# A fifth buffer for gathered expert rows in a one-core decoder block, paid for by rearranged SBUF

## The chip, the cores and the metric

The kernel runs on one core of one Trainium2 chip. The metric is the device time of one execution in microseconds. In the names of the profile PE is TensorE (PEld its weight loads), DVE is VectorE, ACT is ScalarE, POOL is GpSimd and SP is the engine that issues most transfers. PEq, ACTq and SPq are the sequencers of these engines.

## The reference

A decoder block for 512 tokens of width 1024. Two token mixers run side by side on the same normed input, a causal attention with 8 heads and an RWKV-7 recurrence with 8 heads; their outputs are gated and merged. After a second norm comes a mixture of 16,384 tiny experts: each token picks 16 experts for each of 8 heads, so 128 experts per token, and sums their outputs.

```python
mod = silu(c) @ w_ada + b_ada                       # shifts, scales, gates of both halves
h   = modulate(rms_norm(x), sh1, sc1)
proj = h @ w_in
o_mla  = attention(q, k, v)                         # scores + causal mask, softmax, p @ v
o_rwkv = rwkv7(...)                                 # recurrence over 512 steps, in chunks
x = x + gt1 * ((g_mla * o_mla + g_rwkv * o_rwkv) @ w_out)
h = modulate(rms_norm(x), sh2, sc2)
q = h @ w_query                                     # 8 heads, two halves
v1, i1 = top_k(q1 @ sub_keys1, 16); v2, i2 = top_k(q2 @ sub_keys2, 16)
idx, gates = top 16 of the 256 sums, softmax        # 128 experts per token
u, vv = expert_down[idx], expert_up[idx]            # rows of 1024
x = x + gt2 * sum(gates * gelu(h . u) * vv)
```

## The kernel before, in words

The 512 tokens are four blocks of 128, handled in three groups: block 0, block 1, and blocks 2 and 3 together. The first part of the program interleaves three streams: the recurrence of one group (`rwkv`), the attention of the next blocks (`mla_pre`, `mla`), and the tail of a finished group (`tail_a` to `tail_c`, then `select`, which picks the 128 experts of every token). A planner writes the instructions with priorities, and each engine then runs its own list in a fixed order. The list of VectorE is therefore decided before the kernel runs: an instruction that waits holds back everything written after it on that engine.

The experts are computed in two ways.

- **Gathered**, for blocks 0 and 1 (`peer`, L1106). In each of 256 steps GpSimd gathers for 128 tokens one row of 2048 numbers (down row and up row, 1 MB in all) into a buffer `gl`. VectorE multiplies the down half with the token's `h2p` and sums it into `z` (L1119), ScalarE applies gelu and the gate (L1120, L1121), and VectorE adds the up half to `acc` (L1125). There are `GL = 4` such buffers of 8 KB per partition: the gather of step s + 4 waits for the `acc` of step s. These steps are written with a late priority, so the planner drops them into the places where it sees VectorE free.
- **Dense**, for blocks 2 and 3. For each i of 128 rows of experts all activations z are computed as a matrix product (`dense_z`, L1162, tile `ps_z`, weights `u_raw`), multiplied by gates that are zero for unpicked experts, and multiplied by the up rows (`v_raw`) into the accumulators `acc` in PSUM. The first 40 z (`AZ + PZ`) are single products. From i = 40 on, u is split on ScalarE and VectorE into a high part `uh` and a rest `ul` (`hi_lo`, L1147), and z takes 24 matmuls; the product with v is always split and takes 12. The gates are built by `dense_spread` (L1199) in 16 steps: each writes a 1 MB tile `g_` to `gd` in DRAM on ScalarE's queue. `dense` (L1249) reads them back as `G`, one tile for 8 values of i, through `NG = 3` buffers that `g_` and `G` share.

The z from i = 40 on can start before the 128 steps of `dense` do; the names `uh`, `ul` are tiles of the pool `dz`, which is opened when the recurrence is over. The pool `de`, which holds `vh`, `vl`, `ch`, `cl` and `act`, is opened after `dense_spread`, on memory that the tiles of `dense_spread` held.

Before all this, a prologue loads two 4 MB slices of `w_ada` in eight transfers of 1 MB through the same ring `gl`, and VectorE multiplies them (L338, L340) into the scale `hA` without which the first norm cannot be finished. The table of cosines and sines (`rotary`, L377) is made there too, in the tile `rot` of a small ring `u5`.

Of the kernel before, what the change touches and what calls it, by code (L numbers as in the profile page):

```python
# [9 lines left out]
F32 = mybir.dt.float32  # L10
# [9 lines left out]
P = 128  # L20
# [9 lines left out]
GROUPS = ([0], [1], [2, 3])  # L30
DENSE = (2, 3)

GL = 4
PRE = 2
LATE = 1000
ZLATE = 100
ZFIRST = 20
AZ = 32
PZ = 8
NG = 3  # L40
BG = [[0.91, 2, 2, 1.0, 2.2, 2.85, 2.45, 1.0], [1.6, 2.28, 1, 0.58, 0.25, 0.5, 0.13, 0.36]]
ZSTEP = 2
ADA = 1
# [17 lines left out]

CST = {}
_n = 0
for _k, _w in (("ident", P), ("mM", 512), ("mOff", P), ("blk", P), ("causal", P), ("ind2", 2),
               ("sel2", P), ("invf", 16), ("invn", 3), ("invs", 24), ("iota", P)):
    CST[_k] = (_n, _n + _w)
    _n += _w
NCST = _n


def constants():
# [82 lines left out]
def _build(ctx, tc, nc, A, out):  # L154
# [86 lines left out]
        return t.rearrange("p a b -> p (a b)")  # L241


    cst = cp.tile([P, NCST], F32, name="cst")
    cols = cp.tile([P, NCOL], F32, name="cols")
    rows = mp.tile([P, NROW], F32, name="rows")
    posi = cp.tile([P, NB], I32, name="posi")
    nc.sync.dma_start(cols, A["cols"])
    nc.scalar.dma_start(cst, A["cst"])
    nc.scalar.dma_start(posi, A["pos"])  # L250

    def C(k):
        return cst[:, CST[k][0]:CST[k][1]]
# [260 lines left out]
    qT2 = pe.tile([P, 2, 8, P], F32, name="qT2", tag="gl", bufs=GL)  # L514
    G.memset(qT2[96:128], 0.0)
    p2 = pe.tile([P, 2, 512], F32, name="p2", tag="h2p", bufs=1)
    u5 = ring("u5", 512, 2, mp)

    def mla_pre(b):

# [90 lines left out]
    def mla(b):  # L611

        qT = qT2[:, b % 2]
        nk = (b + 1) * P
        ps_o = bank("ps_o", "po", 1)
        sums = small("sums", 8, pl=mp)
        ready = []
        for h in range(9):
            if h < 8:
                ps = psum_m("ps_s")  # L620
                mm(ps[:, :nk], qT[:, h, :], kT[h // 4][:, h % 4, :nk], True, False)
                mm(ps[:, nk - P:nk], ident, C("causal"), False, True)
                mx = small("mx", 1, pl=mp)
                V.tensor_reduce(mx, ps[:, :nk], axis=AX.X, op=ALU.max, negate=True)
                p_ = p2[:, h % 2]
                S.activation(p_[:, :nk], ps[:, :nk], AF.Exp, bias=mx, accum_out=sums[:, h:h + 1])
            if h:
                p_, g = ready
                ps = psum_m("ps_pT")
                for kb in range(b + 1):  # L630
                    PE.transpose(ps[:, kb * P:(kb + 1) * P], p_[:, kb * P:(kb + 1) * P], ident)
                pT = mp.tile([P, 512], F32, name="pT", tag="pT", bufs=2)
                S.copy(pT[:, :nk], ps[:, :nk])
                for kb in range(b + 1):
                    mm(ps_o[:, g * 64:(g + 1) * 64], pT[:, kb * P:(kb + 1) * P], vA[:, kb, g * 64:(g + 1) * 64],
                       kb == 0, kb == b)
            if h < 8:
                ready = p2[:, h % 2], h
            yield
        V.reciprocal(sums, sums)  # L640
        o = u5("o_")
        V.tensor_tensor(split(o, h=8), split(ps_o, h=8), bc(sums, 64, 2), op=ALU.mult)
        ps = psum_m("ps_oT")
        for j in range(4):
            PE.transpose(ps[:, j * P:(j + 1) * P], o[:, j * P:(j + 1) * P], ident)
        oT[b] = sp.tile([P, 4, P], F32, name="oT", tag="oT", bufs=3)
        S.copy(oT[b], split(ps, j=4))
        yield
# [399 lines left out]

    def select(b, tv, tp, iv, sel):

        gates = cp.tile([P, 16, 8], F32, name=f"gates{b}")
        ex = sl("ex", [P, 8, 16])
        V.tensor_tensor(ex, tv, bc(tv[:, :, 0], 16, 2), op=ALU.subtract)
        S.activation(ex, ex, AF.Exp)
        gs = small("gs", 8, pl=cp)
        V.tensor_reduce(gs, ex, axis=AX.X, op=ALU.add)
        V.reciprocal(gs, gs)
        V.tensor_tensor(gates, ex.rearrange("p h k -> p k h"), bc(gs, 16, 1), op=ALU.mult)

        tpi = tp.rearrange("p h k -> p k h").bitcast(I32)  # L1060

        def shr(n):
            t, f = sl("shi", [P, 16, 8], I32), sl("shf", [P, 16, 8])
            V.tensor_scalar(t, tpi, n, None, op0=ALU.logical_shift_right)
            V.tensor_copy(f, t)
            return f


        p4, p2 = shr(4), shr(2)
        pf, t = sl("pf", [P, 16, 8]), sl("t_", [P, 16, 8])  # L1070
        V.tensor_copy(pf, tpi)
        ab = sl("ab", [P, 2, 16, 8], BF16)
        af = sl("af", [P, 16, 8])
        V.scalar_tensor_tensor(af, p4, -16.0, pf, op0=ALU.mult, op1=ALU.add)
        V.scalar_tensor_tensor(t, p2, -12.0, p4, op0=ALU.add, op1=ALU.subtract)
        V.scalar_tensor_tensor(t, pf, 64.0, t, op0=ALU.is_ge, op1=ALU.mult)
        V.tensor_tensor(ab[:, 0], p4, t, op=ALU.add)
        V.scalar_tensor_tensor(t, p2, -4.0, pf, op0=ALU.mult, op1=ALU.add)
        V.tensor_tensor(t, t, af, op=ALU.subtract)
        V.scalar_tensor_tensor(t, pf, 64.0, t, op0=ALU.is_ge, op1=ALU.mult)  # L1080
        V.tensor_tensor(ab[:, 1], af, t, op=ALU.add)
        yield
        idx = cp.tile([P, 2, P], F32, name=f"idx{b}") if b in DENSE else sm("idx", [P, 2, P])
        for n in range(2):
            oh = b4("oh", [P, 16, 16, 8], BF16)
            V.tensor_tensor(oh, bc(ab[:, n], 16, 1), bc(iota16, 16, 2), op=ALU.is_equal)
            V.tensor_tensor(oh, oh, bc(iv[:, n], 16, 2), op=ALU.mult)
            for w in (8, 4, 2):
                V.tensor_tensor(oh[:, :w], oh[:, :w], oh[:, w:2 * w], op=ALU.add)
            V.tensor_tensor(idx[:, n].rearrange("p (k h) -> p k h", k=16), oh[:, 0], oh[:, 1], op=ALU.add)  # L1090
            yield
        gf = gates.rearrange("p k h -> p (k h)")
        if b in DENSE:
            sel[b] = idx, gf
            yield
            return
        V.scalar_tensor_tensor(idx[:, 0], idx[:, 0], 128.0, idx[:, 1], op0=ALU.mult, op1=ALU.add)
        ii = cp.tile([P, P], I32, name=f"ii{b}")
        V.tensor_copy(ii, idx[:, 0])
        sel[b] = ii, gf  # L1100
        yield
# [60 lines left out]
    def dense_z(i):  # L1162
# [13 lines left out]
        if i < AZ + PZ:  # L1176
            zs = ((u, dn["hf"]),)
        else:
            uh = dz.tile([P, D], F32R, name="uh", tag="uh", bufs=2)
            ul = dz.tile([P, D], F32R, name="ul", tag="ul", bufs=2)  # L1180
            hi_lo(uh, ul, u)
            zs = ((uh, hh_), (uh, hl_), (ul, hh_))
        ps = bank("ps_z", "pr", 3)
# [65 lines left out]
    def dense(sel):  # L1249
# [19 lines left out]
        for i in range(P + 1):  # L1269
            if i < P:  # L1270
                if i % SUB == 0:
                    gates_of(i // SUB + 2)
                    if AZ <= i + SUB < AZ + PZ:
                        t = dn["z"].tile([P, SUB, nd], F32, name="A", tag="A", bufs=AZ // SUB)
                        nc.sync.dma_start(t, zd[:, i + SUB - AZ:i + 2 * SUB - AZ])
                        for j in range(SUB):
                            dn["act"][i + SUB + j] = t[:, j]
# [181 lines left out]
```

## Time and profile before

| | us |
|---|---|
| median of 3 runs | 1945.18 (1934.06 to 1948.34) |
| the profiled execution | 1931.73 |
| its span, first to last instruction | 1930.0 |
| PE busy in the span | 1712.6 (89%) |
| DVE busy in the span | 1597.4 (83%) |
| ACT busy in the span | 702.8 (36%) |
| mean DMA rate | 308 GB/s |

The rows further down come from that one execution. Times in them are microseconds from the start of the span; durations at the end of a group row are nanoseconds where the row says "mean". A busy PE is modelled: two matmuls in flight overlap, so the distance from one start to the next tells more than the duration.

### The profile page before, as it was taken

To read this page: it belongs to the slowest core of one execution; us is meant where nothing else is said; L and a number is where in the kernel's file an instruction comes from. 1 tells how busy PE (TensorE), PEld (TensorE's weight loads), DVE (VectorE), ACT (ScalarE), POOL (GpSimd) and SP (SyncE) were. 2 spreads that over 40 slices of the span, in tenths; PEclk is the share of its full clock that TensorE was granted. 3 is DMA by queue.
4 is the path that set the end of the run, shared out by engine and by line. 5 is a ranking of instruction groups with operands and counts; after the bars stand their busy time and mean duration, and the time that the engine had idled before them with its cause. 6 is when DMAs were issued, how large, how long until landed. Compare 5 with 4: busy or idle time off the path is not lost.

```text
span 1930.0 us, 30268 instructions
## 1 busy us (share of the span) xinstructions
PE 1712.6 (89%) x11002; PEld 1465.1 (76%) x11002; DVE 1597.4 (83%) x3724; ACT 702.8 (36%) x1727; POOL 447.9 (23%) x394
## 2 busy tenths in 40 slices
PE   2889999999899999994769868978899999999998
PEld 2667777778787798883458857766689989988897
DVE  6675546458778898887789999977899999999997
ACT  1244233321323322231131123343465555555553
POOL 1210010000232200333322224310133433233230
PEclk9999999899999999996989988998999999999999
DMA  7744755166987975988989978998999999999995
GB/s 299 261 155 146 240 171 181 33 222 211 371 334 266 346 237 180 337 307 301 372 346 354 342 286 307 364 343 331 404 382 404 415 413 415 416 415 413 415 398 201
DMA packets 152642, 595.03 MB, mean 308 GB/s; under 512 B 13854, under 2 KB 47902, under 8 KB 117548
## 3 DMA queue, kind: packets, MB, share of 16 engines
q1 hardware_dynamic: 76768, 287.22, 40.3%
q0 software_dynamic: 39360, 280.51, 37.7%
q10 hardware_dynamic: 36364, 25.36, 4.2%
q8 instruction: 86, 1.41, 0.3%
q14 instruction: 64, 0.52, 0.1%
HBM read 569.96 MB, written 23.09 MB: 307 GB/s over the span
## 4 chain that ended last, share of the span: by engine, by line
issue 31%; PE 28%; DMA 14%; POOL 13%; DVE 12%; ACT 1%; POOLq 0%; SPq 0%; DVEq 0%; ACTq 0%
POOL gl L1116 13%; DMA gl<-in_experts,ii 6%; PE ps_b L234 4%; PE ps_q L234 3%; DMA w_b<-in_w_b 3%; PE ps_gt L234 3%; DVE acc L1125 2%; DVE gl L1119 2%; DMA w_out<-in_w_out 2%; PE ps_m L234 2%; PE ps_ap L234 2%; PE ps_mix L234 2%; DMA w_ada<-in_w_ada 2%; PE ps_y L234 1%; PE ps_s L234 1%
## 5 line engine op out<-in xcount | busy, mean ns | idle before, releaser
L1116 POOL DMA_INDIRECT gl<-in_experts,ii x256 | 393.6, 1537 | 988.5 <-DVE acc L1125 727.1
L1119 DVE SCALAR_TENSOR_TENSOR gl<-gl,h2p 128x1024 f32<-128x1024 f32 x256 | 311.2, 1216 | 51.6 <-DMA gl<-in_experts,ii 51.2
L1125 DVE SCALAR_TENSOR_TENSOR acc<-gl,z,acc 128x1024 f32<-128x1024 f32 x256 | 326.5, 1275 | 5.8 <-ACT z L1121 5.1
L234 PE MATMUL acc<-vh,ch 128*128 128x512 f32 x512 | 198.0, 395 | 11.1 <-ACT ch L1148 9.8
L234 PE MATMUL acc<-vl,ch 128*128 128x512 f32 x512 | 203.0, 397 | 4.3 <-DVE vl L1149 4.3
L234 PE MATMUL acc<-vh,cl 128*128 128x512 f32 x512 | 203.8, 398 | 2.6 <-DVE cl L1149 2.4
L234 PE MATMUL ps_z<-hh,ul 128*128 128x256 f32 x704 | 199.5, 283 | 2.4 <-DVE ul L1149 2.4
L234 PE MATMUL ps_z<-hh,uh 128*128 128x256 f32 x704 | 199.4, 283 | 0.4 <-ACT act L1188 0.4
L234 PE MATMUL ps_z<-hl,uh 128*128 128x256 f32 x704 | 199.6, 283 | 0.0
L1120 ACT ACTIVATE z<-z 128x1 f32<-128x1 f32 x256 | 51.9, 203 | 389.1 <-DVE gl L1119 389.0
L234 PE MATMUL ps_z<-hf,u_raw 128*128 128x256 f32 x640 | 160.2, 391 | 12.6 <-ACT i1T L1222 12.6
L1149 DVE TENSOR_TENSOR vl<-v_raw,vh 128x1024 fp32r<-128x1024 f32 x128 | 156.1, 1219 | 7.8 <-ACT vh L1148 7.6
L234 PE MATMUL ps_gt<-hT,w_b 128*128 128x128 f32 x1024 | 135.2, 285 | 9.8 <-DMA w_b<-in_w_b 7.3
L234 PEld LDWEIGHTS ps_z<-hf,u_raw 128*128 128x128 f32 x640 | 116.9, 195 | 31.6 <-ACT i1T L1222 13.0
L1148 ACT CAST vh<-v_raw 128x1024 fp32r<-128x1024 f32 x128 | 134.1, 1048 | 16.2 <-DMA v_raw<-in_dense 10.1
L234 PEld LDWEIGHTS ps_z<-hh,uh 128*128 128x128 f32 x704 | 134.6, 191 | 7.0 <-issue 3.1
L234 PEld LDWEIGHTS ps_gt<-hT,w_b 128*128 128x128 f32 x1024 | 126.0, 199 | 16.2 <-issue 11.1
L234 PEld LDWEIGHTS ps_z<-hl,uh 128*128 128x128 f32 x704 | 134.8, 192 | 3.1
L234 PEld LDWEIGHTS ps_z<-hh,ul 128*128 128x128 f32 x704 | 134.7, 191 | 2.7 <-DVE ul L1149 2.6
L234 PE MATMUL ps_b<-hT,w_b 128*128 128x128 f32 x896 | 123.2, 287 | 13.9 <-DMA w_b<-in_w_b 11.0
L234 PEld LDWEIGHTS ps_b<-hT,w_b 128*128 128x128 f32 x896 | 112.5, 199 | 24.4 <-issue 12.8
L234 PE MATMUL ps_q<-h2T,w_q 128*128 128x128 f32 x1024 | 125.5, 277 | 1.2 <-DMA w_q<-in_w_query 1.1
(432 smaller groups left out, 3308.5 us busy)
## 6 DMA issues: line engine op xcount, KB each, us to landing
u_raw<-in_dense SPq DMA_DIRECT2D x128, 512.0 KB
v_raw<-in_dense SPq DMA_DIRECT2D x128, 512.0 KB
w_b<-in_w_b SPq DMA_DIRECT2D x90, 512.0 KB
w_q<-in_w_query SPq DMA_DIRECT2D x48, 512.0 KB
w_ada<-in_w_ada SPq DMA_DIRECT2D x32, 512.0 KB
G<-gd SPq DMA_DIRECT2D x16, 1024.0 KB
w_o<-in_w_o SPq DMA_DIRECT2D x24, 512.0 KB
w_out<-in_w_out SPq DMA_DIRECT2D x24, 512.0 KB
```

The source lines that it names most:

```text
L234: PE.matmul(o, l, r, start=start, stop=stop)
L1116: G.indirect_dma_start(out=gl, out_offset=None, in_=A["experts"], in_offset=bass.IndirectOffsetOnAxis(ap=ii[:, s:s + 1], axis=0))
L1119: V.scalar_tensor_tensor(gl[:, :D], gl[:, :D], 1.0, h2, op0=ALU.mult, op1=ALU.mult, accum_out=z[:, 0:1])
L1120: S.activation(z[:, 1:2], z[:, 0:1], AF.Gelu_apprx_tanh)
L1125: V.scalar_tensor_tensor(acc, gl[:, D:], z[:, 1:2], acc, op0=ALU.mult, op1=ALU.add)
L1148: S.copy(hi, x)
L1149: V.tensor_tensor(lo, x, hi.bitcast(F32), op=ALU.subtract)
```

## The change

- The ring `gl` gets five buffers in place of four.
- The 8 KB for it come from the pool `mp` of the attention: the scratch rings `u5` (2 x 2 KB) and `pT` (2 x 2 KB) are gone. Their place is a tile `x5` in the ring `gl` itself, cut into four quarters of 2 KB; two serve as `u5`, two as `pT`. Like the keys and values of the attention, `x5` frees its buffer for gathers when the attention is over.
- The mask `causal` moves from the constants that are kept to a tile of `mp`, with a transfer of its own.
- Gates and indices of blocks 2 and 3 move from the lasting pool to `dz`.
- `uh` and `ul` move from `dz` to `de`.
- `G` and `g_` get two buffers in place of three, and the gates of group j + 1 are asked for at the start of group j, where before those of group j + 2 were.

```diff
-GL = 4
+GL = 5
...
-NG = 3
+NG = 2
...
+NKEPT = CST["causal"][0]
...
-    cst = cp.tile([P, NCST], F32, name="cst")
+    cst = cp.tile([P, NKEPT], F32, name="cst")
+    causal = mp.tile([P, P], F32, name="causal")
...
-    nc.scalar.dma_start(cst, A["cst"])
+    nc.scalar.dma_start(cst, A["cst"][:, :NKEPT])
     nc.scalar.dma_start(posi, A["pos"])
+    nc.scalar.dma_start(causal, A["cst"][:, NKEPT:])
...
-    u5 = ring("u5", 512, 2, mp)
+    x5 = pe.tile([P, 4, 512], F32, name="x5", tag="gl", bufs=GL)
+    turn5 = {"u": 0, "p": 0}
+
+    def half5(kind, shape=None):
+        at = {"u": 0, "p": 2}[kind] + turn5[kind] % 2
+        turn5[kind] += 1
+        t = x5[:, at]
...
+    def u5(name, shape=None):
+        return half5("u", shape)
...
-                mm(ps[:, nk - P:nk], ident, C("causal"), False, True)
+                mm(ps[:, nk - P:nk], ident, causal, False, True)
...
-                pT = mp.tile([P, 512], F32, name="pT", tag="pT", bufs=2)
+                pT = half5("p")
...
-        gates = cp.tile([P, 16, 8], F32, name=f"gates{b}")
+        home = dn["z"] if b in DENSE else cp
+        gates = home.tile([P, 16, 8], F32, name=f"gates{b}")
...
-            uh = dz.tile([P, D], F32R, name="uh", tag="uh", bufs=2)
-            ul = dz.tile([P, D], F32R, name="ul", tag="ul", bufs=2)
+            uh = dn["v"].tile([P, D], F32R, name="uh", tag="uh", bufs=2)
+            ul = dn["v"].tile([P, D], F32R, name="ul", tag="ul", bufs=2)
...
-                    gates_of(i // SUB + 2)
+                    if i:
+                        gates_of(i // SUB + 1)
```

The planner's order moves with it. Three places show how. The first is VectorE in the prologue, from the last multiplication of the first `w_ada` slice to the first row of the recurrence's input (`sh`). Before:

```order
L344 TENSOR_TENSOR hB<-ps_mod,cols 128x8
L398 TENSOR_SCALAR rot<-rot 128x64
L338 TENSOR_SCALAR part<-w_ada,sc 128x1024
L397 TENSOR_TENSOR rot<-rot 128x64
L340 SCALAR_TENSOR_TENSOR part<-w_ada,sc,part 128x1024
...
L407 SCALAR_TENSOR_TENSOR sn<-rot 128x4x16
L408 TENSOR_SCALAR sn<-sn 128x4x16
L340 SCALAR_TENSOR_TENSOR part<-w_ada,sc,part 128x1024 x6
L346 TENSOR_TENSOR hA<-ps_mod,cols 128x8
```

and in the changed kernel, where the table is made in `x5`:

```order
L347 TENSOR_TENSOR hB<-ps_mod,cols 128x8
L341 TENSOR_SCALAR part<-w_ada,sc 128x1024
L343 SCALAR_TENSOR_TENSOR part<-w_ada,sc,part 128x1024 x5
L386 TENSOR_SCALAR x_232<-cst,posf 128x16 x4
...
L349 TENSOR_TENSOR hA<-ps_mod,cols 128x8
...
L411 TENSOR_SCALAR sn<-sn 128x4x16
L507 TENSOR_TENSOR sh<-pr 128x128
```

The table's instructions stood between the multiplications and ahead of `hA`; now 38 of its rows lie between `hA` and `sh`.

The second place is VectorE at the end of the selection for block 3, just ahead of the first step of `dense_spread` (`iota`, then the comparisons `o`). Before:

```order
L1090 TENSOR_TENSOR idx_8753<-oh 128x128
L1089 TENSOR_TENSOR oh<-oh 128x1024
L1211 CAST iota<-cst 128x256
L1089 TENSOR_TENSOR oh<-oh 128x512
L1223 CAST gb<-gT 128x128
L1089 TENSOR_TENSOR oh<-oh 128x256
```

and in the changed kernel:

```order
L1108 TENSOR_TENSOR idx_8681<-oh 128x128
L1107 TENSOR_TENSOR oh<-oh 128x1024
L1137 SCALAR_TENSOR_TENSOR gl,z<-gl,h2p 128x1024
L1107 TENSOR_TENSOR oh<-oh 128x512
L1143 SCALAR_TENSOR_TENSOR acc<-gl,z,acc 128x1024
L1107 TENSOR_TENSOR oh<-oh 128x256
L1137 SCALAR_TENSOR_TENSOR gl,z<-gl,h2p 128x1024
L1108 TENSOR_TENSOR idx_8681<-oh 128x128
L1143 SCALAR_TENSOR_TENSOR acc<-gl,z,acc 128x1024
L1229 CAST iota<-cst 128x256
```

Two whole gather steps stand now where none stood. Counted over VectorE's list up to the first comparison `o`, 129 gather steps are finished before and 135 now.

The third place is the queue of SP where `dense` starts. Before:

```order
L1282 DMA v_raw<-in_dense 128x1024 x4
L1175 DMA u_raw<-in_dense 128x1024 x24
L1282 DMA v_raw<-in_dense 128x1024
L1262 DMA G<-gd 128x2048 x3
L1282 DMA v_raw<-in_dense 128x1024
L1262 DMA G<-gd 128x2048
L1282 DMA v_raw<-in_dense 128x1024 x3
```

and in the changed kernel:

```order
L1301 DMA v_raw<-in_dense 128x1024 x4
L1193 DMA u_raw<-in_dense 128x1024 x20
L1301 DMA v_raw<-in_dense 128x1024
L1280 DMA G<-gd 128x2048 x2
L1301 DMA v_raw<-in_dense 128x1024
L1193 DMA u_raw<-in_dense 128x1024
L1280 DMA G<-gd 128x2048
L1301 DMA v_raw<-in_dense 128x1024
L1280 DMA G<-gd 128x2048
```

Four loads of `u_raw` fewer stand ahead of the first `G`, and two `G` are asked for together in place of three.

## Rows read from the trace of the kernel before

**Rows 1.** Busy time by stage: start:end, length, engines (instructions), clock, DMA share, GB/s

```profile
480.00:660.00 180.00, 164.56 (x1122) 138.36 (x1120) 143.18 (x308) 57.05 (x176) 48.39 (x58) 0.97 0.87 331
660.00:860.00 200.00, 194.05 (x1473) 175.30 (x1474) 176.01 (x564) 58.89 (x182) 42.68 (x40) 1.00 0.75 268
860.00:1010.00 150.00, 96.54 (x501) 72.38 (x500) 119.03 (x238) 35.75 (x117) 50.79 (x37) 0.81 0.89 335
1010.00:1165.00 155.00, 121.77 (x790) 111.31 (x789) 147.32 (x548) 30.51 (x93) 36.59 (x30) 0.91 0.87 321
1165.00:1310.00 145.00, 124.42 (x948) 105.90 (x948) 126.70 (x196) 55.54 (x132) 44.91 (x16) 0.94 1.01 348
1310.00:1450.00 140.00, 131.25 (x561) 104.96 (x562) 127.15 (x191) 71.38 (x130) 27.40 (x19) 0.96 0.97 373
1450.00:1880.00 430.00, 427.36 (x2713) 385.08 (x2712) 424.12 (x558) 237.18 (x472) 150.31 (x86) 1.00 1.02 412
```

**Rows 2.** Instructions of PE in order of time, late in the dense stage

```profile
1871.53 0.40 PE L234 MATMUL acc<-vh,ch 128*128 128x512 f32 x1
...
1874.29 0.28 PE L234 MATMUL ps_z<-hh,uh 128*128 128x256 f32 x1
...
1877.15 0.40 PE L234 MATMUL acc<-vh,ch 128*128 128x512 f32 x1
```

**Rows 3.** VectorE's gate products in order of time: one for each i

```profile
1508.31 0.41 DVE L1287 SCALAR_TENSOR_TENSOR act<-act,G 128x256 f32<-128x256 f32 x1
1513.59 0.41 DVE L1287 SCALAR_TENSOR_TENSOR act<-act,G 128x256 f32<-128x256 f32 x1
1520.02 0.41 DVE L1287 SCALAR_TENSOR_TENSOR act<-act,G 128x256 f32<-128x256 f32 x1
```

**Rows 4.** VectorE's groups, 1500 to 1850: count | busy us, mean ns | idle before

```profile
L1125 DVE SCALAR_TENSOR_TENSOR acc<-gl,z,acc 128x1024 f32<-128x1024 f32 x70 | 89.2, 1274 | 0.0
L1119 DVE SCALAR_TENSOR_TENSOR gl<-gl,h2p 128x1024 f32<-128x1024 f32 x70 | 85.0, 1215 | 5.5 <-DMA gl<-in_experts,ii 5.5
```

**Rows 5.** VectorE's waits, 480:660, 660:860, 860:1010, 1010:1165: total us, times, longest

```profile
DVE gl L1119 <- DMA gl<-in_experts,ii: 12.6, 11, 2.3
DVE gl L1119 <- DMA gl<-in_experts,ii: 8.3, 5, 2.8
DVE gl L1119 <- DMA gl<-in_experts,ii: 11.7, 8, 3.9
DVE gl L1119 <- DMA gl<-in_experts,ii: 7.7, 5, 2.7
```

**Rows 6.** PE's waits, 860 to 1010: total us, times, longest

```profile
PE ps_ynT L893 <- DVE y L887: 18.1, 1, 18.1
```

**Rows 7.** VectorE in the prologue, in order of time, with idle time before

```profile
33.46 7.88 DVE L340 SCALAR_TENSOR_TENSOR part<-w_ada,sc,part 128x1024 f32<-128x1024 f32 x6
45.01 0.17 DVE L346 TENSOR_TENSOR hA<-ps_mod,cols 128x8 f32<-128x8 f32 x1 [3.66 <-PE ps_mod L234]
45.21 0.17 DVE L347 TENSOR_TENSOR hA<-hA,cols 128x8 f32<-128x8 f32 x1
51.58 0.29 DVE L504 TENSOR_TENSOR sh<-pr 128x128 f32<-128x128 f32 x1 [6.21 <-ACT pr L500]
```

**Rows 8.** Busy time by stage in the prologue

```profile
25.00:30.00 5.00, 3.57 (x16) 3.49 (x16) 1.74 (x9) 0.00 (x0) 0.00 (x0) 1.00 1.02 396
35.00:40.00 5.00, 0.00 (x0) 0.00 (x0) 4.89 (x4) 0.00 (x0) 3.04 (x2) 1.00 0.65 264
```

**Rows 9.** ScalarE's queue of transfers from 1174 to 1207, to 1210, to 1213: packets, MB

```profile
q10 hardware_dynamic: 7925, 4.03, 40.7%
q10 hardware_dynamic: 8118, 4.13, 38.2%
q10 hardware_dynamic: 9421, 4.79, 40.9%
```

**Rows 10.** ScalarE in `dense_spread`: fourth write, and first copy of sixth step

```profile
1196.46 1.43 ACTq L1246 DMA_DIRECT2D gd<-g__9001  x1
1207.71 1.07 ACT L1245 COPY g__9138<-ps_G 128x512 f32<-128x512 f32 x2 [3.95 <-PE ps_igT L1221]
```

**Rows 11.** The start of `dense`: last write of gates, first reads, first product

```profile
1292.62 0.52 ACTq L1246 DMA_DIRECT2D gd<-g__9836  x1
1307.09 1.76 SPq L1262 DMA_DIRECT2D G<-gd  x3
1313.07 0.80 PE L234 MATMUL acc<-vh,ch 128*128 128x512 f32 x1 [9.50 <-ACT ch L1148]
```

More of the change, by code (lines that the diff above doesn't have):

```diff
@@ L63 @@
 _n = 0
-for _k, _w in (("ident", P), ("mM", 512), ("mOff", P), ("blk", P), ("causal", P), ("ind2", 2),
-               ("sel2", P), ("invf", 16), ("invn", 3), ("invs", 24), ("iota", P)):
+for _k, _w in (("ident", P), ("mM", 512), ("mOff", P), ("blk", P), ("ind2", 2),
+               ("sel2", P), ("invf", 16), ("invn", 3), ("invs", 24), ("iota", P), ("causal", P)):
     CST[_k] = (_n, _n + _w)
@@ L516, in _build @@
     p2 = pe.tile([P, 2, 512], F32, name="p2", tag="h2p", bufs=1)
-    u5 = ring("u5", 512, 2, mp)
+    x5 = pe.tile([P, 4, 512], F32, name="x5", tag="gl", bufs=GL)
[4 more added lines that the diff above has]
+        t = x5[:, at]
+        if shape is None:
+            return t
+        n = math.prod(shape[1:])
+        assert n <= 512
+        return t[:, :n] if len(shape) == 2 else t[:, :n].rearrange("p (a b) -> p a b", a=shape[1])
+    def u5(name, shape=None):
+        return half5("u", shape)
     def mla_pre(b):
@@ L1082, in select @@
         yield
-        idx = cp.tile([P, 2, P], F32, name=f"idx{b}") if b in DENSE else sm("idx", [P, 2, P])
+        idx = home.tile([P, 2, P], F32, name=f"idx{b}") if b in DENSE else sm("idx", [P, 2, P])
         for n in range(2):
```

## The prediction

> **What bounds the kernel now.** I read the busy time by stage first, because one average over 1930 us says nothing about a program whose stages differ. From 480 to 1165 us the recurrence, the tails and the first gathers are interleaved; from 1165 to 1310 the gates are built; from 1310 on the dense product runs beside the remaining gathers [rows 1]. In the last stage PE, VectorE and the transfers all look full: 427 and 424 of 430 us, and 412 GB/s [rows 1]. A busy PE is modelled, so I then read PE in order of time. One i of the dense stage takes 12 matmuls from 1871.53 to 1874.29, then 24 from 1874.29 to 1877.15, and the next i begins at once [rows 2]: 2.76 + 2.86 = 5.62 us with no gap. The stage itself holds 2713 matmuls in 430 us, at 36 for each i 75.4 of them, so 5.70 us for one i [rows 1]. **The dense stage from i = 40 on runs at PE's own pace**, within 1.5%. VectorE is close behind: it takes 5.28 us for an i with one gather step and 6.43 us for one with half a step more [rows 3]. So a gather step costs VectorE about 2 x 1.15 = 2.3 us of its time, less than the sum of the two durations [rows 4] since instructions overlap.
>
> Earlier it is otherwise. From 860 to 1165 PE has large holes (96.5 of 150 us, 121.8 of 155) while VectorE has 119 and 147 [rows 1], and PE once waits 18.1 us for a VectorE instruction of the recurrence that stands behind gather steps [rows 6]. From 660 to 860 PE is at 194 of 200. Waits of VectorE for gathered rows, which is what a fifth buffer can shorten, come to 12.6, 8.3, 11.7 and 7.7 us in the four stages, 40.3 together [rows 5]; between 1500 and 1850 they are 5.5 us [rows 4].
>
> **The change part by part**, against the profiled execution, which took 1931.7 us. The median of the three runs shown is 13.5 us, or 0.7%, longer; I put the sum on that median.
>
> *Prologue.* The last six multiplications by `w_ada` run back to back from 33.46 to 41.34, `hA` follows at 45.01 [rows 7], while the transfers have already dropped from 396 to 264 GB/s [rows 8]. VectorE is late there, not the loads. The table's rows leave the way: some 30 of them stood between the first multiplication and this burst, at about 0.13 us each, so 4 us. They return behind `hA`, where VectorE now sits idle for 6.21 us [rows 7]; 38 rows at 0.13 are 4.9 us and fit. If they take 0.23 us each because every one needs the one before, they are 8.7 and stick out by 2.5. I take **-4**, between -6 and +3. With the fifth buffer the loads are also asked for earlier; since VectorE is the late one, nothing more.
>
> *Waits for gathered rows.* With five buffers each gather is asked for one `acc` earlier, some 5 us at the pace of the last stage. The longest waits are 2.3 to 3.9 us [rows 5], so one step of lead covers most of them, unless the transfers themselves are the limit: in a run of gather steps VectorE takes one each 2.3 us, and 1.05 MB at the 321 to 335 GB/s of these stages [rows 1] takes 3.2. Five buffers then cover one step more of such a run and no more. Before 860 PE is nearly full and VectorE's waits hardly show: I take 2 of the 20.9 us there, and 12 of the 19.4 behind it: **-14**. Ends: 0 and -40.
>
> *Gather steps that move forward.* Up to the first step of the gate building VectorE's list holds 135 finished steps in place of 129, and twelve in place of thirteen during it. Six steps are 13.8 us. Three of the six come before the query stage, where VectorE has 31 us of holes in 150 [rows 1] but is also the one PE waits for [rows 6]: I count half, 3.5. The other three come where it is nearly full: 6.9. One fewer in the gate building: -2.3. Together **+8**, between 0 and +13.8.
>
> *Gates in two buffers.* A write of 1 MB to `gd` is 2048 pieces of 512 bytes. After 1174 ScalarE's queue had moved 8118 pieces by 1210 and 9421 by 1213 [rows 9]; four writes are 8192. So the fourth write, asked for at 1196.46, landed just after 1210, 13.5 us later, while the first copy of the sixth step came at 1207.71 [rows 10]. With two buffers that copy needs the fourth write's buffer and waits 2.3 us or more. There are 14 such reuses. A step that starts late gives the next write more time, ScalarE is idle for most of a step, and VectorE's two sets of operands run ahead; I take **+4**. Ends: 0, and 16 (every second reuse, none absorbed). At the start of `dense` the first reads wait for the last write, from 1292.62 to 1307.09 [rows 11], with two buffers as with three; group 2 is asked for when group 0 has been used and is needed after the fourth product, which at 2.76 us each leaves some 10 us. Nothing for that.
>
> *Split rows in the later pool.* `uh` and `ul` now lie on memory that the gate building still holds, so products with split rows can't start during it. In PE's list 113 of these matmuls stood ahead of the first `acc` product, and now 38 do. The 75 others filled the hole before 1313.07 [rows 11] and cost nothing; now they come at i = 41 to 43, in the stage that runs at PE's pace: 75 x 2.86 / 24 [rows 2] = **+9**. They cost 0 if PE has slack there, which rows 2 speak against.
>
> *Dense stage.* VectorE's last gather step stands at i = 116 in place of 124, as nine steps more are done when i = 44 is reached. At PE's pace that gives only 8 x (5.70 - 5.62) = **-1**. Ends: -1, and -21 (nine steps at 2.3, if VectorE set the pace). *Mask, constants, x5 in place of two rings:* the scratch keeps two halves of each kind, and PE's order there is the same row for row: 0.
>
> Sum: -4 - 14 + 8 + 4 + 9 - 1 = **+2**, so 1947 on the median's scale.
>
> A rule of the skill bears on the last-but-one term. The Trainium skill (Perfetto Trace Analysis, "Identifying the Most-Contended Engine") says that matmul busy time is a poor measure of how near PE is to its limit, and that the share of weight loads is one to use instead. That share is 385 of 430 us, or 90% [rows 1], which by the rule leaves PE a tenth of slack where VectorE, at 424, has none; the sum would then be that of the first rival. I side with the start-to-start distances [rows 2].
>
> **The rivals.**
>
> *VectorE, not PE, sets the dense stage.* For it: 424 of 430 us busy, and an i with a step and a half takes 6.43 us, longer than PE's 5.62. Against it: PE's gapless starts. Then nine steps fewer are worth 20.7 us in place of 1: 2 - 20 = -18, so 1927. Chance 0.12.
>
> *The waits for rows vanish altogether,* because one buffer more takes each fetch off VectorE's path and PE's holes between 860 and 1165 close with them: -40 in place of -14, so -24 and 1921. Against it: PE is full from 660 to 860, and the runs of steps are fed at 3.2 us each. Chance 0.08.
>
> *Slower: the gate writes hold back ScalarE.* ScalarE's list holds the gelu of the gathered steps behind the copies into `g_`; a copy that waits for a write holds back `z`, and so `acc` on VectorE, which feeds the gate building itself. It decides if a write takes longer than the 11 us or so between its issue and the copy two steps on; rows 9 and 10 show 13.5. With the waits for rows limited by the transfers (0 in place of -14) and 16 in place of 4, the sum is -4 + 0 + 8 + 16 + 9 - 1 = +28, so 1973. Chance 0.17.
>
> *The fifth buffer does nothing,* since five fetches in flight only share the same rate: -4 + 0 + 8 + 4 + 9 - 1 = +16, so 1961. Chance 0.20.
>
> **How the numbers follow.** My forecast has the remaining 0.43: gains and losses that nearly cancel. It is the likeliest, so 1947 is the predicted time. The range takes in the first two rivals' nearer half and the fourth with its worse ends: 1921 to 1970; what lies outside is most of the third (0.14) and some of the second (0.05). About 1% (19 us) is what a measurement can tell from no change: faster than that is the second rival, half of the first, and a little of the forecast's own spread: 0.17. Slower is the third and a little of the fourth: 0.20. Within 1%: 0.63.
>
> **What the profile afterwards would show.** `hA` at about 41 us in place of 45, `sh` at 47 or 48. VectorE's waits for gathered rows from 480 to 1165 at 25 us or less in place of 40. The first `acc` product of `dense` within 5 us of 1313. Start to start on PE still 5.62 us for an i at 1500 and at 1870, and no faster after the last gather step: if an i gets shorter there, VectorE was the limit. The interleaved stage begins at i = 41 and lasts about 9 us longer. ScalarE's copies into `g_` would for the first time wait for the queue of writes. I am wrong if PE turns out to have slack in the dense stage, if the holes from 860 to 1165 close by more than 15 us, or if the gate building takes over 15 us longer than its 145.

## The result, and the profile after

The change runs in 1958.1 us against 1938.9 (medians of 17 runs each). Over all these runs the ratio is **1.009, with a 95% interval of 1.0069 to 1.0111**, so some 17 us slower. The profiled execution of the change took 1964.2 us, at the slow end of its runs (1943 to 1965), the one of before 1931.7, at the fast end of its own (1926 to 1952). Row against row the two differ by 32.5 us, and nearly half of that is the choice of the executions; so below each reading is checked against further profiles.

Busy time by stage of the changed kernel (start:end, length, PE, PEld, DVE, ACT, POOL with instructions, clock, DMA share, GB/s), which answers to [rows 1]:

```profile
480.00:660.00 180.00, 159.90 (x1038) 135.84 (x1038) 135.74 (x307) 52.48 (x162) 50.94 (x56) 0.91 0.82 316
660.00:860.00 200.00, 191.49 (x1426) 171.65 (x1425) 169.40 (x560) 57.10 (x175) 40.92 (x38) 0.97 0.71 251
860.00:1010.00 150.00, 98.90 (x538) 74.56 (x537) 121.38 (x225) 30.92 (x111) 54.27 (x39) 0.80 0.92 359
1010.00:1165.00 155.00, 137.83 (x907) 126.66 (x906) 153.00 (x569) 40.89 (x120) 41.52 (x36) 0.96 0.96 362
1165.00:1310.00 145.00, 108.47 (x806) 90.92 (x806) 130.09 (x220) 46.43 (x120) 39.91 (x17) 0.88 0.92 313
1310.00:1450.00 140.00, 117.43 (x516) 92.05 (x515) 122.72 (x184) 66.79 (x124) 30.00 (x20) 0.91 0.97 368
1450.00:1880.00 430.00, 425.08 (x2689) 380.52 (x2688) 424.36 (x559) 239.10 (x473) 134.33 (x84) 1.00 1.02 413
```

The dense stage is as full as it was. From 480 to 860 PE and VectorE are both busy for less time, at a lower granted clock: that is where this execution fell behind. From there on the windows no longer hold the same work, since everything lies some 25 us later.

VectorE's waits for gathered rows over the whole kernel (total us, times), before and now:

```profile
  DMA gl<-in_experts,ii: 51.2, 42
  DMA gl<-in_experts,ii: 8.5, 7
```

By stage, to set beside [rows 5] (total, times, longest), only 480 to 660 and 860 to 1010 have any; 660 to 860 and 1010 to 1165 have none:

```profile
DVE gl L1137 <- DMA gl<-in_experts,ii: 6.4, 5, 2.3
DVE gl L1137 <- DMA gl<-in_experts,ii: 0.3, 1, 0.3
```

So the fifth buffer did to these waits far more than the prediction gave it (25 us or less left, of 40), and yet the kernel is slower. What grew are other waits. PE's waits for weights from 480 to 1010 added up to 22.1 us before (total, times, longest):

```profile
PE ps_mix L234 <- DMA w_out<-in_w_out: 9.9, 4, 3.1
PE ps_m L234 <- DMA w_o<-in_w_o: 8.0, 3, 3.1
PE ps_gt L234 <- DMA w_b<-in_w_b: 3.1, 3, 2.2
PE ps_q L234 <- DMA w_q<-in_w_query: 1.1, 1, 1.1
```

and now make 38.3:

```profile
PE ps_mix L235 <- DMA w_out<-in_w_out: 12.6, 5, 6.2
PE ps_gt L235 <- DMA w_b<-in_w_b: 11.0, 7, 2.8
PE ps_m L235 <- DMA w_o<-in_w_o: 7.3, 4, 3.7
PE ps_b L235 <- DMA w_b<-in_w_b: 4.0, 2, 2.8
PE ps_q L235 <- DMA w_q<-in_w_query: 3.4, 1, 3.4
```

PE's longest single wait, the 18.1 us of [rows 6], grew as well:

```profile
PE ps_ynT L910 <- DVE y L904: 21.9, 1, 21.9
```

It is 17.8 to 18.1 us in all seven profiles with four buffers and 21.9 to 23.3 in all seven with five. During this wait VectorE starts five multiplications by `h2p` and seven additions to `acc` with four buffers, and eight of each with five: its waits for rows there, 1.0 to 1.3 us with four buffers, are gone in five of the seven with five, but more gather steps stand ahead of the `y` that PE needs.

The prologue answers to [rows 7]: `hA` at 41.79 in place of 45.01, `sh` at 47.92 in place of 51.58.

```profile
41.79 0.17 DVE L349 TENSOR_TENSOR hA<-ps_mod,cols 128x8 f32<-128x8 f32 x1 [3.30 <-PE ps_mod L235]
47.92 0.29 DVE L507 TENSOR_TENSOR sh<-pr 128x128 f32<-128x128 f32 x1 [0.73 <-ACT pr L503]
```

PE in the dense stage, to set beside [rows 2]: an i begins with its first `acc` product, early, and again after VectorE's last gather step, which ended before 1890.

```profile
1499.00 0.40 PE L235 MATMUL acc<-vh,ch 128*128 128x512 f32 x1
...
1504.58 0.40 PE L235 MATMUL acc<-vh,ch 128*128 128x512 f32 x1
...
1899.72 0.40 PE L235 MATMUL acc<-vh,ch 128*128 128x512 f32 x1
...
1905.31 0.40 PE L235 MATMUL acc<-vh,ch 128*128 128x512 f32 x1
```

5.58 us and 5.59 us: **PE's own pace, no faster when VectorE has nothing else to do.**

To compare many profiles I divide the end of the kernel at four VectorE instructions: the cast of the last top-k (`iv`), the first comparison `o` of the gate building, the first gate product `A` of `dense`, and the last addition into `y`. For the change:

```profile
1150.90 0.23 DVE L1054 CAST iv<-i 128x32 bf16<-128x32 uint32 x1
1189.55 0.74 DVE L1252 TENSOR_TENSOR o<-iota,i2T 128x1024 f16<-128x1024 f16 x1
1339.33 1.43 DVE L1306 SCALAR_TENSOR_TENSOR A<-A,G 128x256 f32<-128x256 f32 x4 [8.39 <-DMA G<-gd]
1957.33 1.28 DVE L1330 TENSOR_TENSOR y<-y,x2e 128x512 f32<-128x512 f32 x2
```

and for the kernel before, in a second profile of it (its run took 1945.6 us):

```profile
1139.23 0.23 DVE L1037 CAST iv<-i 128x32 bf16<-128x32 uint32 x1
1176.02 0.69 DVE L1234 TENSOR_TENSOR o<-iota,i2T 128x1024 f16<-128x1024 f16 x1
1323.08 1.10 DVE L1287 SCALAR_TENSOR_TENSOR A<-A,G 128x256 f32<-128x256 f32 x3 [4.84 <-DMA G<-gd]
1938.65 1.29 DVE L1311 TENSOR_TENSOR y<-y,x2e 128x512 f32<-128x512 f32 x2
```

The stretches in all profiles, in us (the ratio is to before, with its interval; "steps" are the gather steps that VectorE's list holds ahead of the first `o`, and those between the first and the last `o`, both counted by their `acc`; the prediction's count of the first is one lower):

| kernel | ratio | steps | `iv` at | to `o` | to `A` | to the end | last three |
|---|---|---|---|---|---|---|---|
| before | 1 | 130, 13 | 1129.8 | 36.7 | 145.6 | 612.7 | 795.0 |
| before, again | | 130, 13 | 1139.2 | 36.8 | 147.1 | 615.6 | 799.4 |
| e4 split rows alone | 1.0033 (1.0007 to 1.0059) | 130, 14 | 1138.1 | 35.0 | 144.9 | 622.8 | 802.7 |
| e3 two gates alone | 1.0064 (1.0033 to 1.0094) | 132, 13 | 1142.3 | 41.3 | 148.1 | 614.1 | 803.5 |
| e6 the same again | 1.0049 (1.0014 to 1.0084) | 132, 13 | 1143.2 | 40.8 | 149.5 | 614.1 | 804.4 |
| e1 change with four buffers | 1.0088 (1.0052 to 1.0125) | 132, 14 | 1149.7 | 39.7 | 148.2 | 617.0 | 804.9 |
| change | 1.0090 (1.0069 to 1.0111) | 136, 13 | 1150.9 | 38.6 | 149.8 | 618.0 | 806.4 |
| e8 change, again | | 136, 13 | 1147.8 | 38.6 | 144.8 | 621.9 | 805.3 |
| e2 change, split rows back | 1.0088 (1.0052 to 1.0124) | 136, 13 | 1139.0 | 38.7 | 156.4 | 607.9 | 803.0 |
| e5 fifth buffer alone | 1.0032 (0.9996 to 1.0068) | 134, 13 | 1144.9 | 34.3 | 152.5 | 610.2 | 797.0 |
| e11 change, 9 steps held | 1.0011 (0.9979 to 1.0044) | 136, 4 | 1138.0 | 38.6 | 123.1 | 629.7 | 791.4 |
| e9 fifth buffer, 10 held | 0.9982 (0.9953 to 1.0011) | 134, 3 | 1137.9 | 34.3 | 114.6 | 636.2 | 785.0 |
| e10 fifth buffer, 5 held | 0.9982 (0.9954 to 1.0010) | 134, 8 | 1144.6 | 34.3 | 116.7 | 628.7 | 779.7 |
| **e12 before, 5 held** | **0.9947 (0.9918 to 0.9977)** | 130, 8 | 1130.0 | 35.8 | 117.3 | 632.4 | 785.5 |

Two things are to be seen at once. Up to `iv` the lists of before, e3, e4, e6 and e12 are the same, and their `iv` still lies anywhere from 1129.8 to 1143.2: a difference of less than 13 us there, between single profiles, says nothing. After `iv` the repeats agree within 5 us, and there the parts of the change can be read off, if they are larger than that. The three stretches after `iv` make 797.0 us in e5, as in before (795.0 and 799.4): with nearly nothing but the fifth buffer changed, no loss shows there.

### The profile page after: what moved, and what is told of

It is laid out like the page before. It is cut to its first block, busy times and chain, and to the rows that moved or that the text cites. A ratio compares the mean times of both kernels' runs of the same rounds, so it can differ in the third digit from the quotient of the medians.

```text
span 1962.5 us, 30290 instructions
## 1 busy us (share of the span) xinstructions
PE 1726.5 (88%) x11002; PEld 1476.2 (75%) x11002; DVE 1598.5 (81%) x3724; ACT 704.4 (36%) x1727; POOL 435.5 (22%) x394
## 5 line engine op out<-in xcount | busy, mean ns | idle before, releaser
L1134 POOL DMA_INDIRECT gl<-in_experts,ii x256 | 378.9, 1480 | 954.3 <-DVE acc L1143 698.4
L235 PE MATMUL ps_z<-hf,u_raw 128*128 128x256 f32 x640 | 160.3, 391 | 19.3 <-ACT i1T L1240 18.1
L235 PE MATMUL ps_b<-hT,w_b 128*128 128x128 f32 x896 | 131.5, 299 | 16.0 <-DMA w_b<-in_w_b 14.1
L235 PEld LDWEIGHTS ps_b<-hT,w_b 128*128 128x128 f32 x896 | 120.8, 211 | 26.1 <-issue 9.9
```

The source lines that it names most:

```text
L235: PE.matmul(o, l, r, start=start, stop=stop)
L1134: G.indirect_dma_start(out=gl, out_offset=None, in_=A["experts"], in_offset=bass.IndirectOffsetOnAxis(ap=ii[:, s:s + 1], axis=0))
```

## The experiments

**Which part costs.** Four kernels, timed against before on one chip.

e1, the change with four buffers for rows:

```diff
-GL = 5
+GL = 4
-    x5 = pe.tile([P, 4, 512], F32, name="x5", tag="gl", bufs=GL)
+    x5 = pe.tile([P, 4, 512], F32, name="x5", tag="x5", bufs=1)
```

> The change with four buffers for gathered rows; the attention's scratch keeps its 8 KB in a buffer of its own, all else as in the change. The lists of the engines are those of the kernel before up to the gate building, apart from the rotary table. Theory A (the fifth buffer itself costs time: the gathers that are fetched ahead hold back the weight loads that PE waits for between 480 and 860 us, and more gather steps lie in stages in which PE is full): most of the loss goes, the ratio to before is 1.002 to 1.005 (about +5 to +9 us, the split rows and the gates remain), and PE's waits for weights from 480 to 1010 us are back at some 22 us from 38. Theory B (the loss comes from what had to make room: split rows, gates in two buffers, scratch): ratio 1.008 to 1.010 as for the whole change.

Measured: 1.0088 (1.0052 to 1.0125), the whole loss. **Theory A falls and theory B holds**: without the fifth buffer the change is as slow as with it, to within some 8 us. The run takes back more than the waits: the table stands again where it stood before (`hA` at 45.36), and the four gather steps that the fifth buffer moves ahead of `o` are back. What theory A said of the weights came true all the same: PE's waits for weights from 480 to 1010 fall back from 38.3 to 24.6 us:

```profile
PE ps_mix L235 <- DMA w_out<-in_w_out: 9.4, 3, 5.9
PE ps_gt L235 <- DMA w_b<-in_w_b: 8.3, 6, 2.1
PE ps_m L235 <- DMA w_o<-in_w_o: 5.4, 3, 2.6
PE ps_q L235 <- DMA w_q<-in_w_query: 1.5, 1, 1.5
```

and VectorE's waits for rows are back at 47.5 us. Over all profiles, PE's waits for weights up to 1165 are 34 to 44 us in the seven with four buffers and 51 to 56 in the seven with five, while VectorE's for rows are 44 to 55 and 4 to 10. The fifth buffer removes some 40 us of waits from one engine and puts 14 on the other, besides the 4 us of PE's longest wait, and the time does not fall.

e2, the change with the split rows in the earlier pool again:

```diff
-            uh = dn["v"].tile([P, D], F32R, name="uh", tag="uh", bufs=2)
-            ul = dn["v"].tile([P, D], F32R, name="ul", tag="ul", bufs=2)
+            uh = dz.tile([P, D], F32R, name="uh", tag="uh", bufs=2)
+            ul = dz.tile([P, D], F32R, name="ul", tag="ul", bufs=1)
```

> The change with the split rows uh and ul in the pool of the gate building again (ul with one buffer, so that they fit). 98 split-row products stand ahead of the first acc product in place of 38. If the split rows cost PE time in the dense stage, 60 x 2.86 / 24 = 7 us come back: ratio to before 1.005 to 1.006 in place of 1.009. If PE has slack there, 1.009 as before. Rival: the split rows are worth the whole loss (some 20 us), ratio 1.000.

Measured: 1.0088 (1.0052 to 1.0124), nothing gained. The table shows why: the stretch after `A` is 10 to 14 us shorter, and the one before it 7 to 12 longer. What the split products save in the dense stage, the gate building loses. The split products do not do that by themselves: the kernel before has 113 of them ahead of the first `acc` product and e4 has 38, and their gate building takes the same time. `ul` has one buffer in e2, and over the whole kernel VectorE waits 6.4 us, in ten waits, to write `ul` until PE has finished a `ps_z` product, a wait that before does not have; it was not tried apart.

e3 and e6, gates of two groups alone, which were timed twice:

```diff
-NG = 3
+NG = 2
...
-                    gates_of(i // SUB + 2)
+                    if i:
+                        gates_of(i // SUB + 1)
```

> The kernel before with gates of two groups in place of three and nothing else. If ScalarE's copies into g_ wait for the queue of writes and hold back the gate building: +4 to +16 us, ratio 1.002 to 1.008. If the two sets of operands of VectorE take up the wait: 1.000, and the gate building keeps its 145 us.

> Gates of two groups alone a second time, since its ratio was known to 0.3% only and its trace shows 2 to 4 us in the gate building where the times say 12. If the term is what the trace shows: 1.002 to 1.004. If it is what the first times said: 1.006.

Measured: 1.0064 (1.0033 to 1.0094) and 1.0049 (1.0014 to 1.0084). **Two gates are the largest part of the loss by these numbers**, though the intervals overlap that of e4 below. ScalarE in order of time in the second of them: the write of a step, and the copies two steps on that need its buffer.

```profile
1206.27 0.52 ACTq L1246 DMA_DIRECT2D gd<-g__8933  x1
1213.07 1.07 ACT L1245 COPY g__9001<-ps_G 128x512 f32<-128x512 f32 x2 [6.53 <-DMA gd<-g__8865]
1214.84 1.07 ACT L1245 COPY g__9001<-ps_G 128x512 f32<-128x512 f32 x2
1215.95 0.52 ACTq L1246 DMA_DIRECT2D gd<-g__9001  x1
1221.99 1.07 ACT L1245 COPY g__9069<-ps_G 128x512 f32<-128x512 f32 x2 [6.07 <-DMA gd<-g__8933]
```

The write asked for at 1206.27 holds the copy at 1221.99: 15.7 us. There are nine such waits, 36.5 us of ScalarE's time; in the two profiles of before there are none and one (3.4 us), and the copy in [rows 10] waited for PE. But the gate building is only 2.4 us longer (148.8 against 146.4, means of two), less than the 5 us by which two profiles of one kernel can differ. The other part stands ahead of it: the stretch from `iv` to `o` is 41 us in place of 36.8, since the planner puts two gather steps more there (132 in place of 130 ahead of the first `o`). 4.3 us for two steps is 2.2 each.

e4, the split rows in the accumulation's pool alone (the diff of e2 on the kernel before, the other way round, with two buffers for both `uh` and `ul`):

> The kernel before with the split rows uh and ul in the accumulation's pool and nothing else: 38 split-row products ahead of the first acc product in place of 113. If PE sets the pace of the dense stage: 75 x 2.86 / 24 = +9 us, ratio 1.0046. If PE has slack there or the last products only fill the same holes: 1.000. Rival: more than 9 (ratio over 1.007), if VectorE's splits of these rows, which come behind the gate building too, are on the path as well.

Measured: 1.0033 (1.0007 to 1.0059), so 1 to 11 us. After `A` the profile has 622.8 us in place of 612.7 and 615.6, +9. The means of e3 and e6 and of e4 add up to 1.009, the 1.0088 of e1: nothing is left over for the scratch in `x5` and the moved mask, which were not tried apart.

e5, the fifth buffer nearly alone: the change with the edit of e2, that of e3 the other way round, and

```diff
-            act = dz.tile([P, nd], F32, name="zp", tag="zp", bufs=2)
+            act = dz.tile([P, nd], F32, name="zp", tag="zp", bufs=1)
```

> The change with gates of three groups and the split rows in the gate building's pool again, so that the fifth buffer (and what goes with it: the scratch in it, the rotary table behind hA, the gather steps moved forward) stands nearly alone; to make it fit, ul and zp have one buffer each. The change against the same with four buffers was 1.0090 against 1.0088. If the fifth buffer is worth nothing and the loss is all in what made room: ratio to before 1.000, between 0.998 and 1.002, gate building (first comparison o to first product with A) at 146 us or less. If two gates cost what their own run says and the split rows nothing in company: 1.002. If the fifth buffer itself costs: 1.006 or more. If it gains once nothing is given up for it: below 0.996.

Measured: 1.0032 (0.9996 to 1.0068). This lies between the case in which the buffer is worth nothing and the one in which it costs, and excludes a gain of more than 0.04%. With two gates and the late split rows taken back, the fifth buffer still earns nothing. But `zp` with one buffer is a price of its own, which PE does not pay in before:

```profile
PE ps_z L235 <- ACT zp L1206: 5.7, 2, 5.0
```

The expected shorter gate building did not show (152.5 us), and this wait, which lies in it, may be part of the reason.

**How much of a profile is the change's.**

> The kernel before once more, for a second profile. If the 23 us by which the first comparison o came later in the changed kernel's profile (1189.5 against 1166.5) are the clock's run-to-run variation, this profile has o anywhere from 1166 to 1184, with dips of the granted clock in other places. If they are the change's: o at 1166 to 1169 again.

> The changed kernel once more, for a second profile. If the loss before the gate building is the change's: first comparison o at 1186 or later again. If it is mostly the clock of that one execution: between 1170 and 1184.

Measured: `o` at 1176.0 and at 1186.4. Both statements hold in part: 23 us between the first two profiles become 10 between the second two. Of these, 2 are the shorter or longer stretch after `iv`; the rest lies ahead of `iv`, where seven profiles with five buffers have a mean of 1143.3 and six with four buffers and the list of before 1137.1, with a spread of about 5 us in each. The 6 us between the means are some two standard errors.

**Where a gather step is free.** If a step ahead of the dense stage costs 2.3 us and PE sets the pace behind it, steps should be held back until then. One small VectorE instruction does it: it copies a mark, made when the last operands of the gate building are, into the tile that the held step writes next.

```diff
+                        if q == len(sel) - 1 and t0 + h0 + HB == n:
+                            dn["built"] = dn["z"].tile([P, 1], F16, name="built")
+                            V.tensor_copy(dn["built"], og[:, 0, 0, 0, 0:1])
...
                 z = pl.tile([P, 2], F32, name="z", tag="z", bufs=4)
+                if b * P + s == HOLD:
+                    V.tensor_copy(z[:, 0:1], dn["built"])
```

On e5, HOLD = 137:

> The fifth buffer nearly alone (as in the run before, ratio 1.003), with one instruction more: gather step 137 waits on VectorE until the last operands of the gate building are made, so that 3 gather steps lie in the gate building in place of 13, and the last gather step stands at i = 126 in place of 118. Theory C (gather steps that lie ahead of the dense stage cost VectorE 2.3 us each, those in the dense stage nothing as long as PE sets its pace): the gate building is 10 x 2.3 = 23 us shorter; 84 split-row matmuls that it hid come back in the dense stage, 84 x 2.86 / 24 = 10 us; net -13, ratio to before 0.996 to 0.998. Rival (VectorE has slack in the gate building, PE or ScalarE sets it): gate building as long as before, ratio 1.008. Rival (VectorE sets the dense stage too): the 23 come back there, ratio 1.003 to 1.008.

On e5, HOLD = 142:

> The same with step 142 held: 8 gather steps in the gate building in place of 13, 68 split-row matmuls fewer ahead of the first acc product, last gather step at i = 122. Theory C: 5 x 2.3 = 11.5 us off the gate building, 8 us back in the dense stage: ratio 1.001 to 1.002. Rivals as for ten steps: 1.006, or 1.003.

On the change, HOLD = 140:

> The whole change with step 140 held: 4 gather steps in the gate building in place of 13, last gather step at i = 124 in place of 115; 25 split-row matmuls fewer ahead of the first acc product. Theory C: 9 x 2.3 = 21 us off the gate building, 3 back in the dense stage, net -18: ratio to before 1.000 in place of 1.009. If the copies into g_ wait for the writes in two buffers whatever VectorE does: no more than half of it, 1.005. If VectorE has slack in the gate building: 1.009 or more.

Measured: 0.9982 (0.9953 to 1.0011), 0.9982 (0.9954 to 1.0010) and 1.0011 (0.9979 to 1.0044). **Theory C holds in its direction**: the change loses 15 us of its 17 by this one instruction, though it keeps two gates and the late split rows; expected were 18. With two gates held steps help no less, so the waits of ScalarE's copies were not the bound there. On e5, from 1.0032, ten held steps bring 10 us where 10 to 14 were expected, and five bring as much, where 2 to 4 were. The hold takes more steps out of the way than was counted: between the first `o` and the first `A` VectorE has 17 in e5 and in the change, but 10 in e10 and 4 in e9 and e11, so seven and thirteen fewer. That it is the steps which count, and not the split products that fall out with them, e4 bears out: it has 75 products fewer ahead of the first `acc` product, one step more, and no shorter gate building.

On the kernel before, HOLD = 138:

> The kernel before, with its four buffers, and step 138 held until the gate building's last operands are made: 8 gather steps in the gate building in place of 13, 89 split-row matmuls fewer ahead of the first acc product (24), last gather step at i = 126 in place of 123. It tells what the fifth buffer adds to the held steps (0.9982 with both). Theory C: 5 x 2.3 = 11.5 us off the gate building, 89 x 2.86 / 24 = 10.6 back in the dense stage: ratio 1.000, and the fifth buffer's earlier steps are what gives the held ones room. If the shorter gate building is worth more than that by itself, as in the two runs with held steps and five buffers (the stretch from the first comparison o to the end 12 to 17 us shorter): 0.993 to 0.995, and the fifth buffer is worth nothing even then.

Measured: **0.9947 (0.9918 to 0.9977), 1929.3 us, half a per cent faster than before and so faster than both kernels**; the rival's number, not theory C's. Its rows:

```profile
1130.04 0.23 DVE L1038 CAST iv<-i 128x32 bf16<-128x32 uint32 x1
1165.87 0.68 DVE L1237 TENSOR_TENSOR o<-iota,i2T 128x1024 f16<-128x1024 f16 x1
1283.17 1.10 DVE L1293 SCALAR_TENSOR_TENSOR A<-A,G 128x256 f32<-128x256 f32 x3 [1.31 <-DMA G<-gd]
1915.54 1.28 DVE L1317 TENSOR_TENSOR y<-y,x2e 128x512 f32<-128x512 f32 x2
```

Busy time from `o` to `A`, in the second profile of before and in e12 (columns as above):

```profile
1176.00:1323.10 147.10, 123.50 (x945) 105.61 (x944) 125.23 (x190) 55.33 (x131) 45.53 (x16) 0.93 1.02 350
```

```profile
1165.90:1283.20 117.30, 110.12 (x847) 91.29 (x847) 105.37 (x167) 46.93 (x103) 28.61 (x8) 0.97 1.03 342
```

VectorE has 19.9 us less work there: eight gather steps went, not five, since the three between the last `o` and `A` moved too (16 before, 8 now), and eight at 2.3 are 18.4; the splits of three rows of u went with them, 3.6 us. PE stands idle for 7.2 us in place of 23.6. After `A` 17 to 20 us come back (632.4). So 9 to 13 us stay, where theory C gave 1 for five steps and would give 8 for eight. Why the stretch shrinks by 28 to 30 us, 10 more than the eight steps cost, and why more than 10.6 come back, is not settled: the order of many instructions moves when one is held. What is settled is that four buffers do it too, so the fifth is not what gives the held steps room.

## Why the prediction was right, and where it was not

The forecast was 1947 us, 2 more than the median of before that it started from; measured is about 17 more. The time lies in the range, and the class, within 1%, is right by a tenth of a per cent, with an interval that reaches beyond it: that much is luck. Step by step:

- *Prologue, -4*: the rows came as forecast. The second row of `hA` (45.21 in [rows 7]) lies at 41.9 to 42.4 in all seven profiles with five buffers and at 45.1 to 45.6 in the seven with four. That the end gains by it is not shown: `iv` came no earlier.
- *Waits for gathered rows, -14*: **the step that failed.** The premise came true beyond what was asked: 51.2 us became 8.5. The conclusion did not. What the fifth buffer does by the prediction's terms is -4 in the prologue, -14 here and some +6 for the four steps that are its own (3.5 for three, 2.3 for one), so -12; e1 and the change have the same ratio to within some 8 us, and e5, with `ul` and `zp` at one buffer each, excludes any gain of a us or more. Which of the three was off by how much is not measured apart, but two things are shown that eat the gain. PE waits longer for weights (54 us against 40, means of seven profiles each); the transfers are fuller there, with 359 to 363 GB/s from 860 to 1165 in both profiles of the change against 321 to 342 in those of before and e1, and that this is what delays the weights is an inference. And the time that VectorE gains is filled with gather steps ahead of work that PE needs: PE's longest wait, which I had read in [rows 6] and priced at half under the steps below, is 4 us longer, not shorter. With 0 in place of -14 the sum is +16, which is the fourth rival's 1961. That rival had the result and the wrong reason: the waits vanished, and it was the rate of the transfers that it thought would keep them.
- *Gather steps that move forward, +8*: right in kind. I laid all six at the fifth buffer's door; four are its own (134 in e5) and two come from the two gates (132 in e3). The price of 2.3 us is borne out from `iv` to `o` where two steps more take 4.3 us: in e3 and e6 against before, and in the change (38.6) against e5 (34.3). The -2.3 for one step fewer in the gate building did not come: thirteen lie there in both kernels, and up to `A` one more. And I had read [rows 3] wrongly: the 6.43 us hold no half step, but a second `ul`, which there comes ahead of the gate product. The rows stand below; the price was right by luck, and the 6.43 was no evidence for the first rival.
- *Gates in two buffers, +4*: the waits of ScalarE's copies came as described, eight in the change's profile and nine in e6, with a gate building 2.4 us longer, which is within its scatter. By the times two gates cost 10 to 12 us, and I can place at most 7 of them (2.4 and the 4.3 of the two steps). I had not seen that this edit moves gather steps too, since I looked at the order of the whole change only.
- *Split rows, +9*: right, 1.0033 alone, +9 after `A`. That they "filled the hole and cost nothing" is borne out by e4, whose gate building is as long without 75 of them (144.9 us against 145.6 and 147.1). In e2, where `ul` has one buffer, putting them back gained nothing.
- *Dense stage, -1*: right. 5.58 and 5.59 us for an i, with gather steps and without. The Trainium skill's rule (Perfetto Trace Analysis, "Identifying the Most-Contended Engine"), by which a weight-load share of 380.52 of 430 us leaves PE a tenth of slack, is not borne out here: VectorE had its last gather step some 12 i's before the end, and PE ran no faster behind it.
- *First `acc` product within 5 us of 1313*: wrong, 1340.24. From `o` it is 150.7 us in place of 146.5 (145.7 in the second profile of the change); the rest had been lost, or fallen to that execution's clock, ahead of `o`.

VectorE in the kernel before, between the second and the third row of [rows 3]. From start to start `acc` takes 1.20 us and the multiplication by `h2p` 1.15, so 2.35 for a gather step; `ul` comes twice.

```profile
1513.93 1.21 DVE L1149 TENSOR_TENSOR ul<-u_raw,uh 128x1024 fp32r<-128x1024 f32 x1
1515.40 1.27 DVE L1125 SCALAR_TENSOR_TENSOR acc<-gl,z,acc 128x1024 f32<-128x1024 f32 x1
1516.60 1.21 DVE L1149 TENSOR_TENSOR vl<-v_raw,vh 128x1024 fp32r<-128x1024 f32 x1
1517.73 1.21 DVE L1119 SCALAR_TENSOR_TENSOR gl<-gl,h2p 128x1024 f32<-128x1024 f32 x1
1518.88 1.21 DVE L1149 TENSOR_TENSOR ul<-u_raw,uh 128x1024 fp32r<-128x1024 f32 x1
```

The first rival (VectorE sets the dense stage) is refuted by the same distances. The second's mechanism happened in part, without its gain: the waits all but vanished. The third's wait happened and was largely absorbed, as e11 shows best. By the letter one sign of being wrong came, since PE is busy for 236.7 us from 860 to 1165 in place of 218.3; but with four buffers (e1) it is 238.7, so that is the shift of the stages and not the fifth buffer.

The Trainium skill (Perfetto Trace Analysis, "Optimization Strategy") says that a gap which repeats on an engine that should be saturated can mean too few buffers for the next tile. It names the wait of [rows 5] rightly, since a fifth buffer took it from 51.2 us to 8.5; that closing it buys time, no run here shows.

## What to carry to other kernels

A wait that ends when a transfer lands is worth its length only if nothing else wants the same transfers and if the freed engine has work that is on the path; ask what the engine will do with the time, and who waits for the queue that is now fuller. Where a planner fills every hole with background work, that work lands in the stages in which its engine is the bound; holding some of it back to the stage that another engine paces was worth 10 us here, and the fifth buffer nothing. Judge each part of a change by its own moved instructions: an edit that only gives up memory made the planner move two steps.

## What the runs showed of the hardware

TensorE's mean granted clock differs from run to run of one kernel, and the time goes with it. In 23 runs of the kernel before on one chip the mean clock lay between 0.946 and 0.961 and the time between 1927 and 1954 us, about 1.6 us less for each 0.001 more (a straight line through the runs, correlation -0.81). Identical lists of instructions were up to 13 us apart at `iv`.

One such loss can be seen in both profiles of the change. PE waited 2.60 us for `w_o` until 579.89 (2.24 us until 581.10 in the other), with the transfers at 420 and 424 GB/s from 577 to 581; the granted clock fell to 0.50, the lower of its two levels (1.2 of 2.4 GHz), and stayed there until about 600. In this stretch PE is nearly always busy and gets through 98 matmuls in 24 us, where e5, with the same list at full clock, has 182 in the same 24:

```profile
578.00:602.00 24.00, 22.11 (x98) 17.97 (x98) 8.94 (x21) 3.65 (x12) 1.67 (x4) 0.57 0.32 117
```

From 560 to 610 the clock is 0.80 in both profiles of the change and 0.93 to 1.00 in the twelve others, five of which have the same list of instructions there as the change (e2, e5, e9, e10, e11). So it is not the order alone. Nor is it the wait alone: in the first profile of before a wait of 2.66 us for `w_o` ended at 606.68, and the clock stayed at 1.00 up to 620; in e5 one of 4.04 us for `w_b` ended at 565.45, and the clock was 0.64 from 566 to 570 and 1.00 from there to 600. What made these two falls so long is not known, nor how often the longer waits are followed by one.
